# One Strassen level in the up projection, and the down projection as a stage of its own

## The chip, the cores and the metric

The kernel runs on one core of a Trainium2 chip (trn2). The time is that of the device for one launch, in microseconds (us), median of three runs. The engines are TensorE (PE; PEld are its weight loads), VectorE (DVE), ScalarE (ACT), GpSimd (POOL) and SyncE (SP), whose queue issues nearly all transfers. PE, DVE, ACT and POOL each work through a list in a fixed order; an instruction whose inputs aren't ready holds up all that stands behind it on its engine.

## The reference

One layer of a model over 1024 prompt tokens and a block of 32 sample tokens, in float32:

```python
h = _rms_norm(x, g_pre_mix)
z = h @ w_in                        # 1024 x 7424: q, k, v, HGRN2's inputs, two gates
ya = _sink_attention(...)           # windows of chunks, 16 heads
yb = _rms_norm(_hgrn2(...)) * silu(ob)
mix = sigmoid(ga) * (ya @ w_br_a) + sigmoid(gb) * (yb @ w_br_b)
x = x + _rms_norm(mix @ w_out, g_post_mix)
hf = _rms_norm(x, g_pre_ffn)
a, u = split(hf @ w_up, 2)          # 1024 x 5632
ac = b_conv + sum(ap[:, j:j + t] * w_conv[j] for j in range(3))   # ap: a behind two earlier tokens
ffn = (gelu(ac) * u) @ w_down       # 2816 x 1024
x = x + _rms_norm(ffn, g_post_ffn)
x = x + (pe @ w_ple) * sigmoid(x @ w_ple_gate)
```

The outputs are x, the last keys and values, the HGRN2 state and the last two rows of ap, for prompt and sample.

## The kernel before, in words

Activations lie by column: 128 features on the partitions, tokens along the columns. There are 1058 columns (1024 prompt, two of padding, 32 sample) in three groups of 384, 384 and 290. To keep float32's precision every factor is split into two float32r parts that add up to it, and each product of a 128x128 weight block with a group's row block is three matmuls: high x high (L189), high x low (L190), low x high (L191), in `product`. Weights go by `plan`, a list in the order of their use. `load_raw` brings a 512 KB tile into one of two raw buffers ("wr"); `load_next` makes the high part by an ACT cast (L170) and the low part by a DVE subtraction (L173).

The stages, with PE's times: attention with the gates (to about 390 us); branch B, HGRN2 (to 912); the products with w_br_a and w_br_b and the output projection (to 1208); the first up products beside the end of x1 (to 1261); ten rounds of up products of two ff tiles and down products of the two before (to about 1950); the last down products beside the per-layer product, and the gate (to the end).

Behind the output projection `z_out` copies each block and adds its squares up; `norm_sums` sums them over partitions on PE (L983), makes 1/sqrt by a chain of small DVE steps (`rsqrt`), and `norm_rows` spreads the result along the columns on PE (L291) and copies it (ACT, L293). `x1_part` then makes x1 row block by row block: two DVE operations (L1041, L1042), the split into parts (L215 on ACT, L216 on DVE), a store and a square. In the up stage `a_out` and `u_out` multiply a block by the norm, `ff_tail` does the three conv taps, gelu, the product with u and the split. `down` adds each pair of ff tiles to an accumulator in SBUF (L1157, DVE).

What sets the order: the program is written engine by engine in Python, and a scheduler orders each engine's list from it; no hand-written table. Buffers limit how far one engine can be ahead of another: six banks of PSUM for products ("mm"), two for transposes and norms ("tr").

## Time and profile before

| What | Value |
| --- | --- |
| median of three runs | 2111.21 us (2109.34 to 2114.71) |
| profiled execution, span | 2111.8 us |
| PE busy | 2086.4 us, 99% |
| DVE busy | 1249.1 us, 59% |
| ACT busy | 799.7 us, 38% |
| POOL busy | 35.7 us, 2% |
| moved by DMA | 160.22 MB, 76 GB/s |

The busy time of an engine is the time in which one of its instructions ran. Matmuls overlap, so a busy PE is read from the distance between starts. A group's row gives line, engine, operation, output and inputs, shape and count, then the busy time and the mean duration of one in ns, then the engine's idle time ahead of them and what ended it. The chain is followed back from the last instruction, at each step to what released it.

### The profile page before, as it was taken

Reading aid. Unit: us, or ns where it says so; the run is one execution under the profiler, and the core shown is the slowest. Engines: PE = TensorE matmul, PEld = TensorE weight load, DVE = VectorE, ACT = ScalarE, POOL = GpSimd, SP = SyncE. Lnnn points to the kernel's source line nnn. Section 1 sums busy time; section 2 is a strip of 40 time slices with the busy share of each in tenths; the row PEclk is TensorE's granted clock in tenths of the full one; section 3 lists DMA queues with packets and bytes.
Section 4 is the critical chain, followed back from the end, with each engine's and each line's share of the span. In section 5 each row is a group of like instructions: output and inputs, shape, how many; then the busy total and the mean of one; then the engine's idle time right before and its main releaser. Section 6 shows DMA issues by size and latency. Waiting matters only on the chain.

```text
span 2111.8 us, 34285 instructions
## 1 busy us (share of the span) xinstructions
PE 2086.4 (99%) x13292; PEld 2059.8 (98%) x13292; DVE 1249.1 (59%) x3204; ACT 799.7 (38%) x1845; POOL 35.7 (2%) x164
## 2 busy tenths in 40 slices
PE   7999999999999999999999999999999999999999
PEld 6999999999999999999999999999999999999998
DVE  6776778356666655652451684555555565556872
ACT  6555556344444444450122454321222122222532
POOL 1000000000000000000000000000000000000000
PEclk9999999999999999999999999999999999999999
DMA  7312212211111111285451221111111112111331
GB/s 223 101 63 71 81 59 71 68 41 45 55 45 48 45 53 53 77 260 165 143 189 59 83 81 40 51 50 41 41 55 46 41 41 61 41 41 53 94 109 53
DMA packets 203601, 160.22 MB, mean 76 GB/s; under 512 B 8798, under 2 KB 194417, under 8 KB 203438
## 3 DMA queue, kind: packets, MB, share of 16 engines
q1 hardware_dynamic: 203086, 157.88, 24.3%
q8 instruction: 105, 1.72, 0.3%
q14 instruction: 58, 0.48, 0.1%
q0 software_dynamic: 352, 0.15, 0.0%
HBM read 121.48 MB, written 36.51 MB: 75 GB/s over the span
## 4 chain that ended last, share of the span: by engine, by line
PE 92%; DVE 5%; DMA 2%; ACT 1%; issue 1%; SPq 0%; ACTq 0%; DVEq 0%
PE mm L189 27%; PE mm L191 27%; PE mm L190 27%; PE tr L448 1%; PE s L814 1%; PE s L421 1%; PE o L470 1%; PE o L471 1%; DVE cb L729 1%; PE s L422 1%; PE o L849 1%; PE s L806 1%; PE o L851 1%; PE tr L508 0%; DVE wl L173 0%
## 5 line engine op out<-in xcount | busy, mean ns | idle before, releaser
L189 PE MATMUL mm<-Ra,wh 128*128 128x384 f32 (+1 forms) x1632 | 531.9, 327 | 4.1 <-ACT gt L282 3.6
L191 PE MATMUL mm<-Ra,wl 128*128 128x384 f32 (+1 forms) x1632 | 529.8, 325 | 0.0
L190 PE MATMUL mm<-Rb,wh 128*128 128x384 f32 (+1 forms) x1632 | 529.4, 325 | 0.0
L189 PE MATMUL mm<-La,wh 128*128 128x384 f32 (+1 forms) x1560 | 523.5, 336 | 0.0
L191 PE MATMUL mm<-La,wl 128*128 128x384 f32 (+1 forms) x1560 | 504.4, 323 | 0.0
L190 PE MATMUL mm<-Lb,wh 128*128 128x384 f32 (+1 forms) x1560 | 503.5, 323 | 0.0
L189 PEld LDWEIGHTS mm<-Ra,wh 128*128 128x128 f32 x1632 | 307.4, 189 | 5.1 <-ACT gt L282 3.8
L190 PEld LDWEIGHTS mm<-Rb,wh 128*128 128x128 f32 x1632 | 308.1, 189 | 0.0
L191 PEld LDWEIGHTS mm<-Ra,wl 128*128 128x128 f32 x1632 | 307.3, 188 | 0.1
L189 PEld LDWEIGHTS mm<-La,wh 128*128 128x128 f32 x1560 | 294.1, 189 | 2.3 <-issue 1.6
L190 PEld LDWEIGHTS mm<-Lb,wh 128*128 128x128 f32 x1560 | 294.5, 189 | 0.2
L191 PEld LDWEIGHTS mm<-La,wl 128*128 128x128 f32 x1560 | 293.8, 188 | 0.0
L170 ACT CAST wh<-wr 128x1024 fp32r<-128x1024 f32 x137 | 143.7, 1050 | 376.9 <-PE mm L190 366.8
L173 DVE TENSOR_TENSOR wl<-wr,wh 128x1024 fp32r<-128x1024 f32 x158 | 193.1, 1223 | 100.1 <-ACT wh L170 95.8
L189 PE MATMUL mm<-act,wh 128*128 128x384 f32 (+1 forms) x528 | 171.1, 324 | 0.0
L190 PE MATMUL mm<-act,wh 128*128 128x384 f32 (+1 forms) x528 | 170.8, 324 | 0.0
L191 PE MATMUL mm<-act,wl 128*128 128x384 f32 (+1 forms) x528 | 170.7, 323 | 0.0
L1157 DVE TENSOR_TENSOR La<-La,mm 128x384 f32<-128x384 f32 (+1 forms) x240 | 122.3, 519 | 71.4 <-PE mm L191 70.5
L432 ACT ACTIVATE sc<-sc,st 128x257 f32<-128x257 f32 (+1 forms) x144 | 69.5, 484 | 92.7 <-DVE st L427 87.7
L190 PEld LDWEIGHTS mm<-act,wh 128*128 128x128 f32 x528 | 99.6, 189 | 0.0
L189 PEld LDWEIGHTS mm<-act,wh 128*128 128x128 f32 x528 | 99.4, 188 | 0.0
L191 PEld LDWEIGHTS mm<-act,wl 128*128 128x128 f32 x528 | 99.4, 188 | 0.0
(292 smaller groups left out, 2536.8 us busy)
## 6 DMA issues: line engine op xcount, KB each, us to landing
wr<-in_w_in_dram SPq DMA_DIRECT2D x58, 512.0 KB, 3.8
wr<-in_w_up_dram SPq DMA_DIRECT2D x44, 512.0 KB, 3.8
wr<-in_w_down_dram SPq DMA_DIRECT2D x22, 512.0 KB, 3.5
ya_d<-ya SPq DMA_DIRECT2D x8, 529.0 KB
x<-in_x_prompt_dram SPq DMA_DIRECT2D x8, 512.0 KB, 5.8
wr<-in_w_br_a_dram SPq DMA_DIRECT2D x8, 512.0 KB
wr<-in_w_br_b_dram SPq DMA_DIRECT2D x8, 512.0 KB, 3.8
wr<-in_w_out_dram SPq DMA_DIRECT2D x8, 512.0 KB, 5.7
```

What stands on the lines that cost most here:

```text
L170: S.copy(hi[:], raw[:])
L173: V.tensor_tensor(lo[:], raw[:], hi[:].bitcast(F32), op=ALU.subtract)
L189: E.matmul(ps, wh, a, start=first and n == 0, stop=False)
L190: E.matmul(ps, wh, b, start=False, stop=False)
L191: E.matmul(ps, wl, a, start=False, stop=last and n == len(ks) - 1)
L421: E.matmul(o, q[:, c:c + P], K1[kv][:, k0:k0 + nk], start=True, stop=False)
L422: E.matmul(o, q[:, c:c + P], K2[kv][:, k0:k0 + nk], start=False, stop=True)
L432: S.activation(sc[:m_, h, b0:e_ + 1], sc[:m_, h, b0:e_ + 1], AF.Exp, bias=st[:m_, 0, h:h + 1], scale=-1.0, accum_out=st[:m_, 1, h:h + 1])
L448: E.transpose(t[:kn, a * 256 + h * m_:a * 256 + (h + 1) * m_], sc[:m_, h, kc:kc + kn], ident[:m_, :m_])
L470: E.matmul(oc, lhs, ph[:kn, a, :2 * m_], start=a == 0, stop=False)
L471: E.matmul(oc, lhs, pl[:kn, a, :2 * m_], start=False, stop=a == len(tl) - 1)
L1157: V.tensor_tensor(dst, dst, b[:, :n], op=ALU.add)
```

## The change

- The tokens lose the two columns of padding: 1056, groups of 384, 384 and 288 up to branch B, then four groups of 264 columns (G4) for the branch products, the output and the per-layer product, and three of 352 (M3) for down and gate.
- The up projection of one ff tile of a and one of u is taken as a 2 x 2 matrix of blocks (a and u, by the halves of the 1024 features) times a 2 x 2 matrix (the halves of the features, by halves of 528 tokens), with seven products of sums of blocks. `build_ops` makes the seven operands of each half of the tokens as whole instructions of four row blocks (1056 columns); `unit_parts` makes the sums of the weights on GpSimd (four additions of 512) and their parts on ACT and DVE. A unit is 7 products x 2 x 4 row blocks x 3 = 168 matmuls of 264 columns, gathered in three accumulators X, Y, Z in PSUM; `after` takes them out.
- x1 is made four row blocks at once, and its squares are added on GpSimd (`x1_squares`). The per-layer product moves from the last down products to the place between output and up stage, and its result goes to DRAM through two buffers (tag "sq").
- The conv and gelu run on all columns at once; the result goes to DRAM (act_d). The down projection runs after all 22 units, for three groups in turn, and adds over all ff tiles in PSUM; its weights are loaded anew for each group, in 96 tiles of six or four row blocks, and `load_chunk` brings act back and splits it. The additions of L1157 are gone.

```diff
-T = 1058
-GR = ((0, 384), (384, 384), (768, 290))
+T = 1056
+GR = ((0, 384), (384, 384), (768, 288))
+H = 264
+G4 = tuple((H * g, H) for g in range(4))
+M3 = 352
...
-    def up_w(ch):
-        return [rows_cols(w_up, 0, h + f * P, P, KT) for f in (2 * ch, 2 * ch + 1) for h in (0, DFF)]
-    def down_w(ch):
-        return [rows_cols(w_down, ch * 256, c * 512, 512, 2) for c in range(2)]
-    for ch in range(NCH):
-        plan += up_w(ch)
-        if ch:
-            plan += down_w(ch - 1)
-    plan += down_w(NCH - 1)
     plan += [rows_cols(w_ple, 0, c * 512, 512, 2) for c in range(2)]
+    n_mix = len(plan)
+    KB = ((0, 6), (6, 6), (12, 6), (18, 4))
+    for _ in range(3):
+        for q in range(2):
+            plan += [rows_cols(w_down, k * P, (4 * q + c) * P, P, n) for k, n in KB for c in range(4)]
...
-    def x1_part(count=0, upto=-1):
...
+    def x1_part(g):
+        rb = oz.tile([P, H], F32, tag="rb", name=nm("rb"), bufs=2)
+        norm_rows(rss[g], T88, rb[:])
+        for i in range(2):
+            zz = z[g][:, 4 * i:4 * i + 4, :].bitcast(F32)
+            x = x1q[g][i]
+            V.tensor_tensor(zz, zz, rb[:].unsqueeze(1).to_broadcast([P, 4, H]), op=ALU.mult)
+            V.tensor_tensor(x[:], x[:], zz, op=ALU.add)
+            dma(x1_d[:, 4 * i:4 * i + 4, H * g:H * g + H], x[:])
+            for k in range(4):
+                S.mul(z[g][:, 4 * i + k, :].bitcast(F32), x[:, k, :], g_ffn[:, 4 * i + k:4 * i + k + 1])
+        x1_squares(g)
+    def x1_squares(g):
+        sq1 = fo.tile([P, H], F32, tag=f"sqz{g}", name=nm("sq1"))
+        for i in range(2):
+            for k in range(4):
+                if i == 0 and k == 0:
+                    S.activation(sq1[:], x1q[g][0][:, 0, :], AF.Square)
+                    continue
+                sq = oz.tile([P, H], F32, tag="sq", name=nm("sq"), bufs=2)
+                S.activation(sq[:], x1q[g][i][:, k, :], AF.Square)
+                G.tensor_tensor(sq1[:], sq1[:], sq[:], op=ALU.add)
+        sqz[g] = sq1
+    def build_ops(p):
+        def at(j):
+            s = where[p][j]
+            ops[p][j] = page(lq if s[0] == "l" else rp, s[1], [P, 2, 4, H], "op")
+            return ops[p][j]
+        q0, q1 = z[2 * p], z[2 * p + 1]
+        b11, b21 = q0[:, 0:4, :].bitcast(F32), q0[:, 4:8, :].bitcast(F32)
+        b12, b22 = q1[:, 0:4, :].bitcast(F32), q1[:, 4:8, :].bitcast(F32)
+        def part(j, src):
+            t = at(j)
+            S.copy(t[:, 0], src)
+            V.tensor_tensor(t[:, 1], src, t[:, 0].bitcast(F32), op=ALU.subtract)
+        part(0, b11)
+        V.tensor_tensor(b11, b11, b12, op=ALU.subtract)
+        V.tensor_tensor(b12, b12, b22, op=ALU.subtract)
+        part(6, b22)
+        V.tensor_tensor(b22, b22, b11, op=ALU.add)
+        part(1, b22)
+        part(2, b21)
+        V.tensor_tensor(b21, b21, b22, op=ALU.subtract)
+        part(3, b12)
+        part(4, b11)
+        part(5, b21)
+    def ple_product(g):
+        if not ple_w:
+            ple_w.extend((next_w(1), next_w(0)))
+        xs = pT.pop(g)
+        for c in range(8):
+            b = block(ple_w[c // 4], slice((c % 4) * P, (c % 4 + 1) * P),
+                      [xs[:, 0, k, :] for k in range(2)], [xs[:, 1, k, :] for k in range(2)],
+                      ((0, 0), (1, 1)), H)
+            t = oz.tile([P, H], F32, tag="sq", name=nm("pl"), bufs=2)
+            S.copy(t[:], b[:, :H])
+            dma(ple_d[:, c, H * g:H * g + H], t[:])
...
+        ws = [next_w(x) for x in range(4)]
+        for g in range(4):
+            for n, w in enumerate(ws):
+                z_out(4 * q + n, g, block(w, ALL, Ra[g], Rb[g], KS, H))
+                if q and g and n == 0:
+                    x1_sums(g - 1)
+                if q and g and n == 2:
+                    x1_part(g - 1)
+                if q and g == 3 and n == 1:
+                    build_ops(0)
...
+    def unit_parts(u):
+        f1, f2 = raw_w.pop(u)
+        sa = wp.tile([P, 2, 4, P], F32, tag="wb", name=nm("sa"), bufs=8)
+        sb = wp.tile([P, 2, 4, P], F32, tag="wb", name=nm("sb"), bufs=8)
+        a11, a12, a21, a22 = f1[:, 0:4, :], f1[:, 4:8, :], f2[:, 0:4, :], f2[:, 4:8, :]
+        s1, s2, s3, s4 = sa[:, 0], sa[:, 1], sb[:, 0], sb[:, 1]
+        def parts(src):
+            t = wp.tile([P, 2, 4, P], F32R, tag="wb", name=nm("wt"), bufs=8)
+            S.copy(t[:, 0], src)
+            V.tensor_tensor(t[:, 1], src, t[:, 0].bitcast(F32), op=ALU.subtract)
+            ready_w.append(t)
+        parts(a11)
+        yield
+        G.tensor_tensor(s1, a21, a22, op=ALU.add)
+        G.tensor_tensor(s2, a11, s1, op=ALU.add)
+        parts(s2)
+        yield
+        parts(a12)
+        yield
+        G.tensor_tensor(s3, a11, a21, op=ALU.add)
+        parts(s3)
+        yield
+        parts(s1)
+        yield
+        parts(a22)
+        yield
+        G.tensor_tensor(s4, a12, s2, op=ALU.add)
+        parts(s4)
...
+    prepare(1)
+    p_cols(0)
+    for g in range(4):
+        if g < 3:
+            p_cols(g + 1)
+        ple_product(g)
+        if g == 0:
+            x1_sums(3)
+            x1_part(3)
+        if g == 1:
+            build_ops(1)
+    octx.close()
...
-    def up(ch):
...
-    def down(ch, act, sums=None):
...
+        V.tensor_tensor(u, u, rbT[:], op=ALU.mult)
+        V.tensor_tensor(u[:, 0:1024], a[:, 0:1024], u[:, 0:1024], op=ALU.mult)
+        V.tensor_tensor(u[:, 1024:T], a[:, 1026:1058], u[:, 1024:T], op=ALU.mult)
+        dma(act_d[f][:], u)
...
+        def mults(i, t, first, ps):
+            n = 7 * u + i
+            if i not in w:
+                w[i] = ready_w[n]
+            for p in ps:
+                for k in range(4):
+                    wh, wl = w[i][:, 0, k, :], w[i][:, 1, k, :]
+                    xh, xl = ops[p][i][:, 0, k, :], ops[p][i][:, 1, k, :]
+                    o = t[:, p, 0:H]
+                    E.matmul(o, wh, xh, start=first and k == 0, stop=False, skip_group_check=True)
+                    E.matmul(o, wh, xl, start=False, stop=False, skip_group_check=True)
+                    E.matmul(o, wl, xh, start=False, stop=k == 3, skip_group_check=True)
+        def v(t, ps):
+            return t[:, ps[0]:ps[-1] + 1, 0:H]
+        def after(i, ps):
+            x, y, zz = v(X, ps), v(Y, ps), v(Z, ps)
+            sl = slice(ps[0], ps[-1] + 1)
+            if i == 0:
+                S.copy(s1c[:, sl], x)
+            elif i == 1:
+                V.tensor_tensor(U2[:, sl], s1c[:, sl], y, op=ALU.subtract)
+            elif i == 2:
+                V.tensor_tensor(ab[:, 2:2 + T].rearrange("p (a h c) -> p a h c", a=2, h=2)[:, sl, 0, :],
+                                x, rb4[:, sl, 0, :], op=ALU.mult)
+            elif i == 3:
+                V.tensor_tensor(nU3[:, sl], y, s1c[:, sl], op=ALU.subtract)
+            elif i == 4:
+                V.tensor_tensor(us4[:, sl, 1, :], nU3[:, sl], zz, op=ALU.subtract)
+            elif i == 5:
+                V.tensor_tensor(us4[:, sl, 0, :], y, s1c[:, sl], op=ALU.subtract)
+            else:
+                V.tensor_tensor(t12[:, sl], U2[:, sl], zz, op=ALU.add)
...
+        order = ((0, X), (1, Y), (2, X), (3, Y), (4, Z), (5, Y), (6, Z))
+        first = (0, 1, 4)
+        for ps in (((0,), (1,)) if u == 0 else ((0, 1),)):
+            for i, t in order:
+                prepare(7 * u + i + AHEAD)
+                mults(i, t, i in first, ps)
+                after(i, ps)
...
+    def load_chunk(g, i):
+        k0, n = KB[i]
+        hi, lo = (page_at(s, [P, 6, M3], "ac") for s in chunk_at[i])
+        for k in range(n):
+            dma(lo[:, k, :].bitcast(F32), act_d[k0 + k][:, M3 * g:M3 * g + M3])
+        for k in range(0, n, 2):
+            src = lo[:, k:k + 2, :].bitcast(F32)
+            S.copy(hi[:, k:k + 2, :], src)
+            V.tensor_tensor(lo[:, k:k + 2, :], src, hi[:, k:k + 2, :].bitcast(F32), op=ALU.subtract)
+        chunk[i] = (hi, lo)
...
+    for g in range(3):
+        for q in range(2):
+            bs = [mm_bank() for _ in range(4)]
+            for i, (k0, n) in enumerate(KB):
+                hi, lo = chunk[i]
+                for c in range(4):
+                    product(bs[c][:, :M3], next_w(), ALL, [hi[:, k, :] for k in range(n)],
+                            [lo[:, k, :] for k in range(n)], tuple((k, k) for k in range(n)),
+                            i == 0, i == 3)
+                    if i == 3:
+                        d_out(g, 4 * q + c, bs[c])
+                if q == 1 and g < 2:
+                    load_chunk(g + 1, i)
```

The first place is PE's list around the norm of the last but one group behind the output projection. Before (L983 are the sums, L291 the rows, `nr` is 1/rms; about 50 products of the first up blocks stand between the two):

```order
L191 MATMUL mm_13520<-Ra_13179,wl_12941 128x384
L983 MATMUL tr_13482<-ones,sqz_12541 128x1 x2
L983 MATMUL tr_13482<-ones,sqz_12541 34x1
L189 MATMUL mm_13520<-Ra_13179,wh_12940 128x384
...
L190 MATMUL mm_13631<-Rb_13180,wh_13353 128x384
L291 MATMUL tr_13607<-ident,nr_13484 128x128 x2
L291 MATMUL tr_13607<-ident,nr_13484 128x34
L191 MATMUL mm_13631<-Ra_13179,wl_13354 128x384
```

And after, on the same engine (L982 the sums, L293 the rows of group 2; mm_14279 is the last output block, `pr` the per-layer input, `pc` its parts by column):

```order
L194 MATMUL mm_14279<-Ra_11980,wl_13601 128x264
L982 MATMUL tr_14131<-ones,sqz_13102 88x1 x3
L293 MATMUL tr_14237<-ident,nr_14133 128x88 x3
L1097 MATMUL tr_14327<-ident,pr_14322 128x88 x3
L1097 MATMUL tr_14333<-ident,pr_14322 128x88 x3
L192 MATMUL mm_14356<-pc_14326,wh_13606 128x264
L192 MATMUL mm_14366<-pc_14326,wh_13606 128x264
```

The rows of the norm no longer have products between them and the sums.

The second place is DVE's list in the same stretch. Before (`rst` and `nr` are the steps of the norm, the others x1's row blocks):

```order
L1041 SCALAR_TENSOR_TENSOR La_12534<-La_12534,gph,rb_13421 128x384
L204 SCALAR_TENSOR_TENSOR rst_13492<-rsb_13491 128x3
L985 TENSOR_SCALAR nv_13546<-tr_13545 128x3
L205 TENSOR_TENSOR rst_13492<-rst_13492,nv_13483 128x3
L216 SCALAR_TENSOR_TENSOR Rb_13428<-La_12534,gvec,Ra_13427 128x384
L206 SCALAR_TENSOR_TENSOR nr_13484<-rst_13492,rsb_13491 128x3
L997 TENSOR_TENSOR sq_2236_13429<-sq_2236_13429,sq_13509 128x384
```

And after (L1076 and L1067 are the sums and the low parts of the up operands `op`, made from z):

```order
L985 TENSOR_SCALAR nv_14132<-tr_14131 88x1
L1076 TENSOR_TENSOR z_13090<-z_13090,z_13091 128x1056
L203 TENSOR_SCALAR rsb_14140<-nv_14132 128x3
L1012 TENSOR_TENSOR sqz_13103<-sqz_13103,sq_14179 128x264
L204 TENSOR_SCALAR rsb_14140<-rsb_14140 128x3
L1067 TENSOR_TENSOR op_14191<-z_13091,op_14191 128x1056
L207 SCALAR_TENSOR_TENSOR rst_14141<-rsb_14140 128x3
L1067 TENSOR_TENSOR op_14198<-z_13091,op_14198 128x1056
L208 TENSOR_TENSOR rst_14141<-rst_14141,nv_14132 128x3
L1067 TENSOR_TENSOR op_14201<-z_13090,op_14201 128x1056
L209 SCALAR_TENSOR_TENSOR nr_14133<-rst_14141,rsb_14140 128x3
```

The steps of the norm now alternate with instructions of 1056 columns instead of 384.

The third place is ACT's list at the per-layer product's copies. Before, beside the last down products (L1231 the copies, kept in SBUF; y is the gate):

```order
L1231 COPY ple_20762<-mm_20813 128x290
L212 CAST Ra_20475<-La_14048 128x384
L1231 COPY ple_20762<-mm_20827 128x290
L996 ACTIVATE sq_20720<-La_14050 128x290
L996 ACTIVATE sq_20745<-La_14050 128x290
L293 COPY rb_20698<-tr_20699 128x384
```

And after, between the last copy of group 0 and the first copies of group 1 (L1112 the copies, L1035 the scalings of x1 of group 3, L1043 and L1046 the squares, L1066 the casts of operands):

```order
L1112 COPY pl_14433<-mm_14426 128x264
L1035 ACTIVATE z_13093<-x_2276_13917,gvec 128x264 x3
L1035 ACTIVATE z_13093<-x_2277_13919,gvec 128x264 x4
L1043 ACTIVATE sq_2368_14478<-x_2276_13917 128x264
...
L1066 CAST op_14617<-z_13092 128x1056
L1046 ACTIVATE sq_14498<-x_2277_13919 128x264
L1112 COPY pl_14525<-mm_14518 128x264
L1066 CAST op_14607<-z_13093 128x1056
L1112 COPY pl_14535<-mm_14528 128x264
```

The copies that free PE's banks stand behind x1's scalings and the operands' casts.

More of the change, by code (lines that the diff above doesn't have):

```diff
@@ L1003, in layer_kernel @@
[L1003 to L1014 removed]
+    z = [page(lq, g, [P, 8, H], "z") for g in range(4)]
@@ L1120, in up @@
[L1120 to L1131 removed]
+        n = T + 2
+        a = fp.tile([P, T + 2], F32, tag="a", name=nm("a"), bufs=2)
@@ new lines, in layer_kernel, with page_at @@
+    for u in range(NF):
+        up_unit(u)
+    chunk_at = (("l4", "r3"), ("l6", "r5"), ("l7", "r6"), ("r0", "r7"))
+    def page_at(s, shape, name):
+        return page(lq if s[0] == "l" else rp, s[1:], shape, name)
+    chunk = {}
+    def load_chunk(g, i):
[8 more added lines that the diff above has]
+        chunk[i] = (hi, lo)
@@ L1315 @@
+            x2_part(0, g)
+            for c in range(4):
+                if q == 0 and g == 0 and c == 0:
+                    x2_start(2)
+                if q == 0 and g == 0 and c == 2:
+                    x2_rows(2)
+                b = block(ws[c], ALL, xh[g], xl[g], KS, M3)
+                x2_part()
+                late.append((g, 4 * q + c, y_out(g, 4 * q + c, b)))
+                if len(late) > 1:
+                    y_done(*late.pop(0))
+    for l in late:
+        y_done(*l)
 _INS = ['x_prompt', 'x_sample', 'cache_win_k', 'cache_win_v', 'state_hgrn', 'cache_ffn_conv',
```

617 lines of the change are left out of this document (275 added, 342 removed).

## The prediction

> **What bounds the kernel now.** I read the page's engine line first, then the span in slices, then the chain that ended last.
>
> ```profile
> span 2111.8 us, 34285 instructions
> PE 2086.4 (99%) x13292; PEld 2059.8 (98%) x13292; DVE 1249.1 (59%) x3204; ACT 799.7 (38%) x1845; POOL 35.7 (2%) x164
> ...
> PE   7999999999999999999999999999999999999999
> ...
> DVE  6776778356666655652451684555555565556872
> ACT  6555556344444444450122454321222122222532
> ...
> PEclk9999999999999999999999999999999999999999
> ...
> PE 92%; DVE 5%; DMA 2%; ACT 1%; issue 1%; SPq 0%; ACTq 0%; DVEq 0%
> ```
>
> TensorE is busy in every slice but the first, at full clock, and 92% of the chain is PE. Work taken from PE is time taken from the span, as long as nothing else makes PE wait. The table by stage shows where a helper could become that:
>
> ```profile
> 912.00:1208.00 296.00, 292.42 (x1804) 291.87 (x1802) 126.42 (x238) 82.06 (x154) 0.20 (x2) 0.99 0.48 145
> 1208.00:1261.00 53.00, 53.00 (x337) 52.35 (x337) 47.85 (x142) 27.43 (x52) 0.00 (x0) 1.00 0.28 92
> 1261.00:1950.00 689.00, 689.00 (x4265) 689.00 (x4264) 379.24 (x709) 173.07 (x269) 2.01 (x20) 1.00 0.15 46
> ```
>
> (Start and end, length, then busy time of PE, PEld, DVE, ACT, POOL, then clock, DMA share, GB/s.) Between 1208 and 1261 us, where the output projection hands over to the first up products, DVE is busy 47.85 of 53 us and PE still does not wait. That stage is the narrow place. In the 689 us of up and down chunks, DVE is at 55%.
>
> **Prices.** Matmuls are pipelined, so the spacing of starts counts, not the recorded 0.34 us.
>
> ```profile
> 1499.83 0.34 PE L191 MATMUL mm<-Ra,wl 128*128 128x384 f32 x1
> ...
> 1503.17 0.29 PE L189 MATMUL mm<-Ra,wh 128*128 128x290 f32 x1
> ...
> 1503.98 0.30 PE L189 MATMUL mm<-Ra,wh 128*128 128x290 f32 x1
> ```
> ```profile
> 301.23 0.28 PE L470 MATMUL o<-ph,Vs 128*128 128x256 f32 x1
> 301.35 0.28 PE L471 MATMUL o<-pl,Vs 128*128 128x256 f32 x1
> 301.47 0.27 PE L470 MATMUL o<-ph,Vs 128*128 128x256 f32 x1
> ```
>
> From 1499.83 to 1503.17 there are 19 starts of 384 columns: 0.1758 us each. Then 6 of 290 columns in 0.81 us: 0.135. A product of 256 columns takes 0.12. Between these, 264 columns are worth 0.123 us and 352 columns 0.162; a triple over all tokens costs 2 x 0.1758 + 0.135 = 0.4866 us before, 4 x 0.123 = 0.492 in four groups of 264, and 3 x 0.162 = 0.486 in three of 352.
>
> ```profile
> L173 DVE TENSOR_TENSOR wl<-wr,wh 128x1024 fp32r<-128x1024 f32 x158 | 193.1, 1223 | 100.1 <-ACT wh L170 95.8
> ...
> L213 DVE TENSOR_TENSOR pl<-tr,ph 128x512 fp32r<-128x512 f32 x56 | 38.0, 688 | 2.8 <-ACT ph L212 1.9
> ...
> L1157 DVE TENSOR_TENSOR La<-La,mm 128x384 f32<-128x384 f32 x160 | 86.7, 552 | 55.6 <-PE mm L191 55.6
> ...
> L1157 DVE TENSOR_TENSOR La<-La,mm 128x290 f32<-128x290 f32 x80 | 35.6, 455 | 15.8 <-PE mm L191 14.9
> ...
> L205 DVE TENSOR_TENSOR rst<-rst,nv 128x3 f32<-128x3 f32 x27 | 4.2, 157 | 0.2
> ```
> ```profile
> 1206.59 0.56 DVE L1042 TENSOR_TENSOR La<-La,xT 128x384 f32<-128x384 f32 x1
> 1207.05 0.46 DVE L997 TENSOR_TENSOR sqz<-sqz,sq 128x290 f32<-128x290 f32 x1
> 1207.42 0.56 DVE L1042 TENSOR_TENSOR La<-La,xT 128x384 f32<-128x384 f32 x1
> ```
> ```profile
> 1207.17 0.62 ACT L215 ACTIVATE Ra<-La,gvec 128x384 fp32r<-128x384 f32 x1 [1.26 <-DVE La L1042]
> 1207.70 0.51 ACT L993 ACTIVATE sq<-La 128x384 f32<-128x384 f32 x1
> 1208.11 0.60 ACT L215 ACTIVATE Ra<-La,gvec 128x384 fp32r<-128x384 f32 x1
> ```
>
> A two-input DVE operation lasts about 0.15 us plus 1.05 ns a column (1223, 688, 455 ns), and the next independent one starts some 0.09 us before it ends (0.46 after 0.56). So DVE passes 1056 columns in 1.18 us, 1024 in 1.14, 512 in 0.60, 264 in 0.35. ACT passes 384 columns with a scale in 0.53 and without in 0.41; scaled, 264 take 0.42 and 0.32, and 1056 plain ones about 1.0. A step that depends on the one before pays all of its 0.157.
>
> **The change, part by part.**
>
> Up products. Before: 44 weight tiles x 24 x 0.4866 = 513.8 us. After: 22 units x 168 products x 0.123 = 454.6. Gain 59.2. The three projections in groups of 264: 24 tiles x 24 x (0.492 - 0.4866) = +3.1; the per-layer product +0.3; 58 input tiles without two columns about -1.2; down and gate at 0.486 instead of 0.4866: nothing. PE in all: **-57**, with +1 for a fourth group's norm and more small transposes.
>
> The 240 additions of L1157 (86.7 + 35.6 = 122.3 us of DVE) leave. DVE was covered there, so that is worth nothing by itself; it makes room for the new evacuations.
>
> Up units in steady state. Each takes PE 168 x 0.123 = 20.7 us. DVE does, in that time, 7 weight remainders of 512 (4.2), 6 evacuations of 528 (3.7), the last pieces L1277 and L1280 (0.8), three copies (0.3), two taps of 1058 (2.5), two products with the norm and u (2.4): 13.9 us, 67%. The kernel before shows PE without a wait at 55%. What is new is GpSimd with four additions of 512 a unit. No row has a two-input GpSimd operation; the nearest are these:
>
> ```profile
> 9.93 0.31 POOL L570 TENSOR_SCALAR_AFFINE_SELECT cm<-cm 128x128 f32<-128x128 f32 x1
> 10.17 0.19 POOL L377 MEMSET qa<- 128x96 f32 x1
> ```
>
> 0.24 us from start to start for 128 columns with one input, so 512 need 0.7 (as on DVE) to 1.9 us (twice 0.96), or 3 to 8 us a unit: GpSimd itself keeps up. If DVE stood still meanwhile it would need 17 to 22 of 20.7 us, so a unit loses 0 to 0.7 us. I take 0.3 in most units, near the lower end because 13.9 leaves room: **+8** with the first unit's half products, bounds 0 and +15.
>
> Hand-over from the output projection to the up stage. Here whole four-block instructions of 1056 columns and the seven operands of each half (11 instructions of 1.18 for each half) come onto DVE, and PE's order shows nothing to do beside them. I follow PE.
>
> (a) Behind the last output block stand L982 and L293 of group 2 with no product between. L982 waits for the last square of group 2. From the norm rows of group 1 (L293, with 3.1 blocks or 9.2 us of PE still to come) DVE has eight instructions of 1056, two of 1024 and one of 264 to pass, with 0.46 for the copy of the rows: 9.4 + 2.3 + 0.35 + 0.46 = 12.5. PE waits 3.5 at least, 9 if DVE also waits for ACT's 18 scalings, squares and casts. Between L982 and L293 DVE has five more of 1056 (5.9), two of 264 (0.7), three of 512 (1.8) and the 12 small steps, of which the last stand alone (1.5): 9.9, up to 12. I take 6.5 + 11 = **17.5**, bounds 13.5 and 21.
>
> (b) The first per-layer product waits for its lower parts, which are put behind four x1 instructions: 0.46 + 4 x 1.18 + 0.7 = 5.9, less 1.3 of transposes and five first products: **+4.6**, bounds 3 and 7.
>
> (c) Per-layer products have six banks; their copies stand in ACT's order behind the x1 scalings, squares and casts. Group 0: 8 x 0.42 + 9 x 0.32 + 2 x 1.0 + 0.6 = 8.9 and DVE's 2.4 ahead of them, against PE's lead of 1.3 + 6 x 0.74 = 5.7: about 5. Group 1: from L293 of group 3, 0.46, four x1 instructions 4.7, the last scalings 1.7, six of the second half's operands 7.1, a cast and a copy 2, in all 16, against PE's 4: 12. Together **+17**, bounds 8 and 22.
>
> (d) The copies go out to DRAM through two buffers:
>
> ```profile
> ta_d<-gt SPq DMA_DIRECT2D x16, 192.0 KB, 2.1
> ```
>
> With 0.4 for the copy and a little under 2.1 for 132 KB a buffer turns in about 2.4 us, a block in 1.2, where PE needs 0.74: for groups 2 and 3, 16 x 0.46 = 7.4, and a backlog of about five blocks that the first up product waits for, since it takes the same banks: **+13**, bounds 5 and 18. Smaller waits (sums of groups 0 and 3): **+3**, 0 to 6.
>
> The hand-over: 55, bounds 30 and 74.
>
> Down stage. The weights come three times, through two raw buffers. The gate stage before shows such a ring's turn:
>
> ```profile
> 1999.96 1.14 DVE wl L173
> ...
> 2001.13 4.37 DMA wr<-in_w_ple_gate_dram
> ...
> 2005.52 1.06 ACT wh L170
> ...
> 2006.62 0.44 PE mm L189
> ```
>
> 1.14 + 4.37 + 1.06 and the gaps make 6.6 us for a buffer, 3.3 for a tile of 512 KB. The new tiles have 384 KB (72 of them) and 256 KB (24). If the load shrinks nearly with its size (3.6 and 2.9), a tile comes every 2.7 and 2.0 us, and PE needs 18 x 0.162 = 2.92 and 1.94: covered but for a little. If loads stay at 4.37, since act chunks travel beside them, it is 3.0 and 2.8: 72 x 0.1 + 24 x 0.9 = 29 us. I take **+6**, bounds 0 and 29, near the lower end because a load with less to move has no row that makes it as slow as a full one. The cover is the ring itself; were it gone, each late tile would stop PE at once, since four banks wait for it. Stores of act, loads of chunks and x1 go on SP's queue; their issues stand between weight loads, and that is in the same bounds. Moving the per-layer product ahead leaves the end of the kernel shorter of work, not longer, and I cost it at nothing.
>
> Sum: -57 + 1 + 8 + 55 + 6 = +13 us. The span is 2111.8 us, and the median of the three runs 2111.21, so one execution stands for them. **2124 us.**
>
> A rule that could change this: the Trainium skill, page "SBUF — State Buffer", section "SBUF: two separate sides", says that GpSimd and a DVE instruction with two inputs in SBUF exclude each other for a whole instruction. By its page "GPSIMD Engine Reference", section 3.1, an addition of 2048 columns takes GpSimd 4497 ns, so 264 would be an estimated 0.6 us. No row of this trace shows two-input work on GpSimd beside DVE. By the two together the 28 additions of squares in the hand-over would be taken out of DVE's time there, some 17 us, and the sum would be +30 instead of +13.
>
> **The rivals.**
>
> 1. Faster. The waits of the hand-over hide each other: PE, stopped in (a), lets DVE and ACT run ahead, and then (c) and (d) find their banks empty. For it: in the same place before, 47.85 of 53 us of DVE were hidden, and the chains in (c) start from work that (a) has already delayed. Against it: the order puts (b) and (c) behind x1 work that cannot start before L293. Left would be the serial minimum of (a), 13.5, and 8 for the rest: -57 + 1 + 21.5 + 0 + 0 = -34.5, **2077 us**. It decides once the hand-over costs less than 42 us.
>
> 2. GpSimd holds DVE up, in the hand-over and in the units. In the hand-over 28 additions of 264 at 0.24 / 128 x 264 = 0.5 to twice that: 14 to 28 us, of which DVE has nearly no slack to absorb any. In the units up to +15 instead of +8. About +13 + 20 + 7 = +40, **2151 us**. For it: the hand-over's squares are waited for by ACT in order. Against: POOL's rows before are too short to show anything.
>
> 3. The down stage is bound by its ring: +29 instead of +6, **2147 us**. For it: the gate stage before waits on the same ring (the DMA of 4.37 above was in the chain); against: smaller tiles.
>
> 4. No change: the hand-over at 45 and the rest near its lower ends, **2111 us**.
>
> That the change does not do what it says is no rival: the order has 168 products of 264 columns for each unit.
>
> **How the numbers follow.** My case 0.38; rival 1: 0.25; rival 2: 0.15; rival 3: 0.10; rival 4: 0.12. Runs before differ by 5.4 us, so about 0.3% (6.3 us) is what can be told from no change. Slower: 0.38 + 0.15 + 0.10 = 0.63; same 0.12; faster 0.25. The predicted time is that of my case, whose own range is 2112 to 2138. The range for all cases reaches from 2074, a little below rival 1's time, to 2160, a little above rival 2's; that leaves out some 0.1 at each end.
>
> **What the profile after would show.** PE in the up stage: starts of 264 columns 0.123 us apart and a unit every 21 us; if 0.135 or more, the gain is 10% of 455 us smaller. Idle time of PE just before L982 and L293 of group 2 (17 us), released by DVE; before the per-layer products, released by ACT; before the first up product. In the units DVE near 67% busy and PE's wait under 0.7 us. In the down stage, waits of PE on casts of weights below 10 us in all. I am wrong if the hand-over has under 42 us of PE's idle time, or if GpSimd's additions take over 2 us each.

## The result

The changed kernel takes 2135.24 us (median of four runs, 2134.1 to 2138.28), the kernel before 2111.1: 1.011 times as long, 95% interval 1.009 to 1.0129. The profiled execution spans 2133.8 us.

The page of the changed kernel:

```profile
span 2133.8 us, 37571 instructions
...
PE 2042.0 (96%) x14474; PEld 2007.0 (94%) x14474; DVE 1318.4 (62%) x3131; ACT 902.3 (42%) x2029; POOL 195.3 (9%) x264
...
PE   7999999999999999999999567999999999999998
...
PEclk9999999999999999999999778999999999999999
...
PE 78%; DVE 8%; DMA 6%; issue 3%; ACT 3%; POOL 1%; SPq 0%; ACTq 0%; DVEq 0%; POOLq 0%
```

PE is busy for 44 us less than before, and the span is 22 us longer. Slices 23 to 25, from about 1174 to 1334 us, are where it went: PE is half busy, and its granted clock falls with it. That is the hand-over from the output projection to the up stage. Who ends PE's waits there (engine and line that waits, who ended it, us in total, times, longest):

```profile
PE mm L192 <- ACT pl L1112: 18.6, 4, 12.0
PE tr L293 <- DVE nv L980: 11.7, 2, 10.7
PE tr L982 <- DVE sqz L1012: 11.6, 3, 8.7
PE st L1249 <- ACT pl L1112: 7.4, 1, 7.4
PE tr L1097 <- DVE pc L216: 3.2, 1, 3.2
```

Between two up products in the steady state (first and tenth of a row of starts):

```profile
1499.83 0.29 PE L1249 MATMUL st<-op,wt 128*128 128x264 f32 x1
...
1500.92 0.28 PE L1249 MATMUL st<-op,wt 128*128 128x264 f32 x1
```

Nine starts in 1.09 us: 0.121 us for 264 columns. In parts of the hand-over the same size starts only every 0.22 us, called half pace here:

```profile
1238.40 0.42 PE L192 MATMUL mm<-pc,wh 128*128 128x264 f32 x1
1238.62 0.42 PE L193 MATMUL mm<-pc,wh 128*128 128x264 f32 x1
```

It is the clock: the profile grants 0.50 from 1185.0 to 1188.3 us and from 1262.0 to 1266.8, and 1.00 from 1188.5 to 1199. Half pace follows waits. PE was idle for 2.2 us up to 1183.55 us, ran 1.4 us at full pace and then 3.3 us at half pace; after the wait that ended at 1261.78 half pace lasted 5.1 us. Summed over all starts from 1175 us to the end of the first unit (the first pair of ff tiles in the up stage), products took 14.1 us more than at 0.121, and the waits were 58.9 us. Such sums of waits are taken here from one start of PE to the next, less one product; the idle time that the profile gives, as in the list above, is 56.5 us in the same stretch.

The account of the 24 us, from the first product of the branch stage to the end (1195.5 us before, 1219.5 after): a unit of the up stage has a pitch of 20.35 us. Before, a triple over all tokens took 0.485 us on the mean from 1261 to 1950 us (the prediction's row gave 0.4866), so that a unit's worth took 44 x 24 x 0.485 / 22 = 23.28: -64. Products of 352 columns start 0.160 us apart, a triple 0.480, which gives some -4 in down and gate. The waits of the hand-over and the half pace: +73. One wait in the second unit: +1. The down stage: 12 us of waits, and some 4 for half pace behind them: +16. The columns of padding give -1 and more, and the kernel before lost 2 us to half pace and short waits in these stages itself. That makes about +19; the last 5 are not assigned. The account adds up PE's time. It doesn't show that each term, taken away alone, would shorten the kernel by its size; that is what the experiments are for.

### The profile page after: what moved, and what is told of

It is laid out like the page before. It is cut to its first block, busy times and chain, and to the rows that moved or that the text cites. A ratio compares the mean times of both kernels' runs of the same rounds, so it can differ in the third digit from the quotient of the medians.

```text
span 2133.8 us, 37571 instructions
## 1 busy us (share of the span) xinstructions
PE 2042.0 (96%) x14474; PEld 2007.0 (94%) x14474; DVE 1318.4 (62%) x3131; ACT 902.3 (42%) x2029; POOL 195.3 (9%) x264
## 4 chain that ended last, share of the span: by engine, by line
PE 78%; DVE 8%; DMA 6%; issue 3%; ACT 3%; POOL 1%; SPq 0%; ACTq 0%; DVEq 0%; POOLq 0%
PE mm L192 16%; PE mm L193 16%; PE mm L194 16%; PE st L1251 6%; PE st L1249 6%; PE st L1250 6%; DMA wr<-in_w_down_dram 3%; DVE wl L176 1%; PE tr L449 1%; POOL sq L1047 1%; PE s L815 1%; ACT wh L173 1%; PE s L422 1%; PE o L471 1%; DVE cb L730 1%
## 5 line engine op out<-in xcount | busy, mean ns | idle before, releaser
L192 PE MATMUL mm<-La,wh 128*128 128x384 f32 (+1 forms) x1368 | 458.8, 336 | 0.0
L1249 PE MATMUL st<-op,wt 128*128 128x264 f32 x1232 | 349.8, 284 | 8.6 <-ACT pl L1112 7.4
L1251 PE MATMUL st<-op,wt 128*128 128x264 f32 x1232 | 351.0, 285 | 0.0
L1250 PE MATMUL st<-op,wt 128*128 128x264 f32 x1232 | 349.0, 283 | 0.0
L176 DVE TENSOR_TENSOR wl<-wr,wh 128x1024 fp32r<-128x1024 f32 (+2 forms) x188 | 198.0, 1053 | 175.6 <-ACT wh L173 171.0
L173 ACT CAST wh<-wr 128x1024 fp32r<-128x1024 f32 (+2 forms) x167 | 149.4, 895 | 283.4 <-DMA wr<-in_w_down_dram 119.5
L1249 PEld LDWEIGHTS st<-op,wt 128*128 128x128 f32 x1232 | 232.7, 189 | 9.1 <-ACT pl L1112 7.7
L1250 PEld LDWEIGHTS st<-op,wt 128*128 128x128 f32 x1232 | 232.7, 189 | 0.0
L1251 PEld LDWEIGHTS st<-op,wt 128*128 128x128 f32 x1232 | 232.1, 188 | 0.0
L192 PE MATMUL mm<-ac,wh 128*128 128x352 f32 x528 | 172.0, 326 | 3.2 <-ACT wh L173 3.2
L194 PE MATMUL mm<-ac,wl 128*128 128x352 f32 x528 | 171.4, 325 | 2.9 <-DVE wl L176 2.6
L193 PE MATMUL mm<-ac,wh 128*128 128x352 f32 x528 | 170.1, 322 | 0.0
L192 PE MATMUL mm<-Ra,wh 128*128 128x264 f32 x512 | 146.4, 286 | 1.1 <-ACT gt L284 1.1
L193 PE MATMUL mm<-Rb,wh 128*128 128x264 f32 x512 | 145.8, 285 | 0.0
L194 PE MATMUL mm<-Ra,wl 128*128 128x264 f32 x512 | 145.7, 285 | 0.0
```

Source lines behind the costliest of these rows:

```text
L173: S.copy(hi[:], raw[:])
L176: V.tensor_tensor(lo[:], raw[:], hi[:].bitcast(F32), op=ALU.subtract)
L192: E.matmul(ps, wh, a, start=first and n == 0, stop=False)
L193: E.matmul(ps, wh, b, start=False, stop=False)
L194: E.matmul(ps, wl, a, start=False, stop=last and n == len(ks) - 1)
L1249: E.matmul(o, wh, xh, start=first and k == 0, stop=False, skip_group_check=True)
```

## The experiments

The profiles are compared by three stretches: from the first branch product to the first up product, to the last up product, to the end. The first varies less than the whole, since the runs start that stage 909 to 920 us into the span.

| Kernel | to first up product | up stage | to the end | time, us |
| --- | --- | --- | --- | --- |
| changed | 381.5 | 456.4 | 381.6 | 2135.24 |
| squares on DVE | 376.0 | 456.8 | 389.1 | 2137.49 |
| places for per-layer products | 359.8 | 460.0 | 384.7 | 2120.67 |
| added products | 382.1 | 456.8 | 386.1 | 2139.02 |
| third raw buffer | 382.0 | 456.4 | 366.0 | 2118.44 |
| third buffer, squares on DVE | 377.8 | 454.9 | 366.6 | 2112.61 |
| third buffer, up sums on DVE | 380.9 | 456.0 | 367.4 | 2114.16 |
| third buffer, no squares | 355.3 | 456.3 | 366.2 | 2092.01 |
| third buffer, places | 359.3 | 458.8 | 366.2 | 2097.91 |
| third buffer, added products | 383.9 | 454.8 | 366.5 | 2121.39 |
| all repairs | 354.1 | 458.2 | 366.6 | 2091.91 |
| all repairs, added products | 354.8 | 459.8 | 364.5 | 2092.04 |

**Squares on DVE.**

```diff
-                G.tensor_tensor(sq1[:], sq1[:], sq[:], op=ALU.add)
+                V.tensor_tensor(sq1[:], sq1[:], sq[:], op=ALU.add)
```

> The changed kernel with the squares of x1 (line 1047, 28 additions of 264 columns) added on DVE instead of GpSimd. Theory GpSimd-chain: in the hand-over these additions took 0.76 us alone and up to 1.65 us beside two-input DVE work, ACT's squares wait for them and the operands' casts and the copies of the per-layer product stand behind those; without them PE's idle time between 1181 and 1301 us falls from 59 us to about 52, and with some of the lost clock back the time falls by 6 to 10 us, to 2125 to 2129. Rival DVE-bound: DVE is the limit of the hand-over, and 28 x 0.35 = 10 us more on it lengthen it: 2140 to 2146.

Measured: 2137.49 us, ratio to before 1.012 (1.0095 to 1.0145). The first up product came 5.5 us sooner, but the stretch behind the last up product was 7.5 us longer: PE's waits in the down stage were 20.1 us here and 11.6 in the profile of the changed kernel. The time lies between the two forecasts and decides neither theory; the down stage had to be quieted first.

**A third raw buffer for the down weights.**

```diff
-        raws.append(wp.tile([P, kt, n], F32, tag="wr", name=nm("wr"), bufs=2))
+        third_ring = len(raws) >= n_mix + 16 and (len(raws) - n_mix) % 3 == 2
+        pool, tag, bufs = (ring3[0], "wr3", 1) if third_ring else (wp, "wr", 2)
+        raws.append(pool.tile([P, kt, n], F32, tag=tag, name=nm("wr"), bufs=bufs))
...
-            yrs[g] = ep.tile([P, 3, 256], F32, tag="yr", name=nm("yr"), bufs=4)
+            yrs[g] = ep.tile([P, 3, 256], F32, tag="yr", name=nm("yr"), bufs=3)
```

> The changed kernel with a third raw buffer for the down weights (from the 17th tile on; one buffer less for rows of the output, in the gate stage). Theory ring: PE's 12 us of waits in the down stage come from the turn of two raw buffers (load, cast, subtraction); with three they fall below 3 us, and the time by 8 to 10 us, to 2125 to 2128. Rival transfers: the loads are slow because act chunks, x1 and weights share the DMA engines (0.6 busy there); then a third buffer changes under 3 us.

Measured: 2118.44 us, 1.0026 times before (1.0011 to 1.0041), 17 us faster than the changed kernel: more than either theory said. PE's waits in the down stage before the edit (`wh` and `wl` are the parts of the down weights, `sqd` the squares for the norm behind it), and after it:

```profile
PE mm L192 <- ACT wh L173: 3.2, 6, 1.1
PE tr L982 <- DVE sqd L1344: 2.7, 1, 2.7
PE mm L194 <- DVE wl L176: 2.6, 6, 0.5
```

```profile
PE tr L985 <- DVE sqd L1348: 0.8, 1, 0.8
PE tr L296 <- DVE nr L212: 0.4, 1, 0.4
```

So the ring of two buffers was the limit, not the transfers alone. The waits on weights lay between 1821 and 1846 us and between 1929 and 1936, where `load_chunk` brings act for the next group: there the casts and the subtractions came late. With the third buffer the stretch to the end is 364.5 to 367.4 us in all kernels, 15.6 shorter here than in the changed kernel. About 10 of it are waits; the half pace behind them (3.7 us from 1935.72 and 5.4 from 2026.20 in the changed kernel) is likely a part of the rest.

**The squares again, with the third buffer.**

> Squares of x1 on DVE instead of GpSimd again, this time with the third raw buffer, so that the down stage's waits (11.6 to 20.1 us in the profiles so far) do not cover the result. Theory GpSimd-chain: 2118.4 - 6.6 = about 2112 us. Rival: the earlier start of the up stage was a matter of the one profile, 2116 to 2121.

Measured: 2112.61 us, ratio to before 0.9997 (0.9985 to 1.0009). That is what the GpSimd theory gave: 5.8 us less than with the third buffer alone. DVE got 28 more additions and the hand-over was shorter, so it is not DVE's load that sets it. The rows show how it goes. GpSimd in the changed kernel:

```profile
L1159 POOL TENSOR_TENSOR sa<-wu,sa 128x512 f32<-128x512 f32 x22 | 46.0, 2089 | 1.7
L1047 POOL TENSOR_TENSOR sq<-sq,sq 128x264 f32<-128x264 f32 x28 | 31.7, 1133 | 842.2 <-ACT sq L1046 840.6
L1158 POOL TENSOR_TENSOR sa<-wu 128x512 f32<-128x512 f32 x22 | 29.9, 1359 | 210.8 <-PE st L1251 196.4 <-ACT wt L1153 9.1 <-DVE wt L1154 5.2
```

ACT, behind such an addition each time (in brackets its idle time and what ended it):

```profile
1257.91 0.42 ACT L1046 ACTIVATE sq<-x 128x264 f32<-128x264 f32 x1 [1.29 <-POOL sq L1047]
1258.24 1.05 ACT L1066 CAST op<-z 128x1056 fp32r<-128x1056 f32 x1
1259.63 0.42 ACT L1046 ACTIVATE sq<-x 128x264 f32<-128x264 f32 x1 [0.34 <-POOL sq L1047]
1261.35 0.38 ACT L1112 COPY pl<-mm 128x264 f32<-128x264 f32 x1 [1.29 <-POOL sq L1047]
```

With two places for the squares, ACT makes one square for each addition, and the copy that frees PE's bank stands at the end of that row. In all, ACT stood idle for 11.5 us behind GpSimd's additions between 1181 and 1301 us. DVE's instructions beside GpSimd's also took longer there, an estimated 5 us together (nine additions of 264 columns 0.67 us on the mean instead of 0.43, four sums of 1056 columns 1.7 to 2.0 instead of 1.25). The edit takes away most of both, so how much of the 5.8 us either one holds isn't shown.

**Places for the per-layer products.**

```diff
-    ple_w = []
+    ple_w, pages = [], []
...
-            t = oz.tile([P, H], F32, tag="sq", name=nm("pl"), bufs=2)
-            S.copy(t[:], b[:, :H])
-            dma(ple_d[:, c, H * g:H * g + H], t[:])
+            if c == 0:
+                pages.append(page(*((rp, 5), (rp, 7), (lq, 2), (lq, 3))[g], [P, 8, H], "pl"))
+            t = pages[-1][:, c, :].bitcast(F32)
+            S.copy(t, b[:, :H])
+            dma(ple_d[:, c, H * g:H * g + H], t)
```

> The changed kernel with eight places for each group's per-layer products (in pages of SBUF that are free there) instead of two buffers shared with the squares. Theory buffers: the copies wait for the stores of the two buffers, which costs PE part of the wait in group 1, the waits in groups 2 and 3 and the 7.4 us before the first up product: 17 us of idle time less, and some clock back, 2110 to 2118. Rival order: the copies come late because they stand behind x1's scalings and the operands' casts in ACT's order; the buffers then change less than 4 us, 2131 to 2139.

Measured: 2120.67 us (ratio to before 1.0035, 1.0021 to 1.0049), 14.6 less than the changed kernel, a smaller gain than the theory of the buffers forecast (2110 to 2118 us) and a far larger one than its rival's. The first up product came 21.7 us sooner. In the hand-over of the changed kernel ACT had waited most of all for the stores out of the two buffers:

```profile
ACT pl L1112 <- DMA ple_d<-pl: 19.7, 14, 4.7
```

With the places that wait is gone. PE's longest waits then:

```profile
PE tr L293 <- DVE nv L980: 11.1, 3, 10.7
PE mm L192 <- ACT pl L1114: 11.0, 2, 10.5
PE tr L982 <- DVE sqz L1012: 10.0, 2, 7.8
PE tr L1097 <- DVE pc L216: 5.8, 2, 3.2
PE st L1251 <- ACT Sp L1262: 3.1, 1, 3.1
```

The wait in front of the first up product (7.4) and those of the small copies are gone; one of 10.5 on a copy is left, that of group 1. So more than half of the 26 us that PE waited for copies was the two buffers, and the order on ACT is the likely rest. Part of the gain came back: the last line is a new wait in the first unit, where ACT's copy (L1262) waits 3.9 us for a store of these places, and the stretch of the up stage grew from 456.4 to 460.0 us. With the third raw buffer as well:

> Places for the per-layer products and the third raw buffer, squares still on GpSimd. If the 22.9 us that the places brought forward stand by themselves: 2118.4 - 22.9 = 2095.5 us, within 4; then the squares on DVE add only 4 us in the kernel with all repairs (2091.9), not 6.6. Rival: part of them came back as waits of the down stage in that profile, 2099 to 2106.

Measured: 2097.91 us, 0.9934 (0.992 to 0.9948), 20.5 less than with the third buffer alone, as the first theory said.

**Squares left out.** Of the eight squares of x1 in each group seven are left out here, with their additions; the norm ahead of the up projection is that of one row block.

```diff
                 if i == 0 and k == 0:
                     S.activation(sq1[:], x1q[g][0][:, 0, :], AF.Square)
-                    continue
+                continue
```

> With the third raw buffer, and seven of the eight squares of x1 of each group (ACT) with their additions (GpSimd) left out, so that the norm ahead of the up projection is that of one row block. Theory: the squares stand in ACT's order ahead of the operands' casts and of the per-layer copies, so the first up product comes 20 to 28 us sooner, 2090 to 2098 us. Rival, DVE-bound: the hand-over is set by DVE's 1056-column instructions, which are all still there; under 8 us sooner.

Measured: 2092.01 us, 26 less than with the third buffer alone. DVE's 1056-column instructions were all there, so they alone don't set the hand-over. PE's waits in front of the norm's sums and rows fell to 8.1 us, from 25.5 in the changed kernel. The squares also share the two buffers of the per-layer copies, so this run doesn't tell ACT's order from the use of the buffers.

**Up sums on DVE.** The four sums of each unit's weights (s1 to s4) are made by V instead of G.

> With the third raw buffer, the four sums of up weights of each unit on DVE instead of GpSimd. If GpSimd's additions (1.3 to 2.1 us each) hold DVE up in the units, DVE without them would be no busier and the units no longer; if DVE has room for 4 x 0.6 us more, the pitch of a unit stays at 20.35 us either way, and the time is 2115 to 2120. Rival: DVE is at its limit with 90% of a unit, and the pitch rises to 20.6 or more, 2124 or later.

Measured: 2114.16 us, 1.0002 times before (0.999 to 1.0014), some 4 us less than with the third buffer alone. The edit isn't shown to have brought these 4 us: the three stretches of the two profiles sum up to the same 1204 us, and 2.3 us of the difference lie ahead of the branch stage. The pitch of a unit stayed at 20.35 us. From 1400 to 1700 us (busy time of PE, PEld, DVE, ACT, POOL), first this kernel, then the changed one:

```profile
1400.00:1700.00 300.00, 300.00 (x2479) 300.00 (x2478) 246.47 (x417) 106.36 (x148) 1.49 (x15) 1.00 0.25 79
```

```profile
1400.00:1700.00 300.00, 300.00 (x2479) 300.00 (x2478) 232.93 (x354) 106.40 (x149) 90.24 (x74) 1.00 0.25 79
```

DVE took the sums at 82% with PE never waiting. Its busy time rose by only 13.5 us, though 60 additions of 0.69 us, 41 us of work, came onto it. The reason is in its longest instructions, the two conv taps of a unit, with the sums on GpSimd (L1224 and L1225) and on DVE (L1227 and L1228):

```profile
L1225 DVE SCALAR_TENSOR_TENSOR a<-ab,cvec,a 128x1058 f32<-128x1058 f32 x22 | 47.5, 2160 | 0.7
L1224 DVE SCALAR_TENSOR_TENSOR a<-ab,cvec,a 128x1058 f32<-128x1058 f32 x22 | 39.0, 1773 | 12.4 <-ACT a L1223 12.4
```

```profile
L1227 DVE SCALAR_TENSOR_TENSOR a<-ab,cvec,a 128x1058 f32<-128x1058 f32 x22 | 29.1, 1321 | 1.3 <-ACT a L1226 1.2
L1228 DVE SCALAR_TENSOR_TENSOR a<-ab,cvec,a 128x1058 f32<-128x1058 f32 x22 | 29.0, 1316 | 0.0
```

The taps run beside GpSimd's additions and take 1.3 us more in each unit. So GpSimd does hold DVE up in the units, but DVE has room for it: PE waited once, 1.2 us in the second unit, and not at all with the sums on DVE.

**Added products.** 220 products (138 in the last of the three kernels) whose results are thrown away stand in PE's waits.

```diff
+    def idle_work(n, d=None):
+        d = d or tr_bank()
+        for _ in range(n):
+            E.matmul(d[:, :H], ws[3][0][:, 0, :], Ra[3][0], start=True, stop=True)
```

> The changed kernel with 220 more products of 264 columns whose results are thrown away (about 27 us at full clock), put into PE's waits of the hand-over: 60 before the last output block, 80 behind the sums of group 2, 80 before the seventh per-layer block of group 1. Theory clock: PE's granted clock falls after its idle stretches (0.22 us from start to start of a product of 264 columns instead of 0.121), which costs 14 us; with PE kept busy the clock stays up, and the time falls by 6 to 12 us, to 2123 to 2129, though PE has more to do. Rival: the clock falls for another reason, or idle time is all that counts; then the time stays, or rises by what the added products delay, 2134 to 2150.

> The 220 thrown-away products in the waits again, now with the third raw buffer. In the first such run the first up product came 2.3 us sooner than without them, though PE had 26.6 us more to do, and products at half pace took 14.3 us of real work instead of 27.3; the time was covered by the down stage's waits. Theory clock: 2 to 7 us below the kernel with the third buffer alone (2118.4), 2111 to 2116 us. Rival: the added products delay as much as the clock gives, 2117 to 2121.

> The kernel with all repairs (2091.9 us), with 138 thrown-away products of 264 columns in the two waits that are left around the sums of group 2 (13 and 5 us): 100 ahead of the sums, 38 behind them. Theory clock: behind these waits about 7 us of products ran at half pace, so 3 us come back, 2087 to 2090. Rival: no gain, or a loss where the products do not end before the norm is ready, 2091 to 2098.

Measured: 2139.02 us; with the third buffer 2121.39 (without them 2118.44); with all repairs 2092.04 (without them 2091.91). The stretch to the first up product was 382.1, 383.9 and 354.8 us, against 381.5, 382.0 and 354.1 without them. So the added products gained nothing, though PE's waits there fell from 58.9 to 38.2 us in the first and from 37.5 to 21.0 in the last. The clock did rise in the first: from 1181 to 1320 us the granted clock was 0.88 instead of 0.74, and the time did not fall, since PE had 26.6 us more to do. In the last, products lost 11.3 us to half pace instead of 8.4: the waits that were left, some 2 to 4 us each, were again followed by half pace. The theory that the lost clock can be bought back with thrown-away products so falls. That half pace follows waits stays as an observation; how much shorter the hand-over would be at full clock, nothing here shows, since a slower PE ahead of a wait may only shorten that wait.

**All repairs.** Squares on DVE, places, third raw buffer, and the squares of the last group behind the per-layer products.

> All repairs together: squares of x1 added on DVE, eight places for each group's per-layer products, a third raw buffer for the down weights from the 17th tile on, and the squares of the last group of x1 put behind the per-layer products. Separately these brought the first up product forward by 6.6 us (squares on DVE) and 22.9 us (places), and shortened the part behind the last up product from 381.6 to 366.0 us (third buffer). Theory that they are separate waits: 2118.4 - 22.9 - 6.6 = 2089 us, within 5, which is 1% faster than the kernel before. Rival that the first two remove the same wait: 2095 to 2100.

Measured: 2091.91 us, 0.99 times before (0.9883 to 0.9916): 1% less than the kernel before, and 2% less than the changed one. PE's longest waits in its hand-over:

```profile
PE tr L985 <- DVE sqz L1015: 13.5, 2, 13.2
PE tr L1101 <- DVE pc L219: 6.2, 2, 3.2
PE tr L296 <- DVE nv L983: 5.8, 3, 5.3
```

The hand-over still holds 37.5 us of waits. The effects add up nearly: 2118.44 - 20.5 - 5.8 = 2092. The fourth edit, the moved squares of the last group, has no run of its own; this sum leaves nothing for it.

## Why the prediction was right, and where its terms were off

The direction and the cause were right: the up stage gained more than 2% of the span, and the hand-over took it back. Forecast 2124, measured 2135; it lay in the range, and near the upper end of my case's own (2112 to 2138). That the sum came so close is in part luck, as its terms show:

- *Up products, -59.* Too small: a product of 264 columns takes 0.121 us, not 0.123, and the gain was 64. The price was read off a line between single rows of 256 and 290 columns, and the product lies below that line.
- *(a), 17.5.* The waits in front of L982 and L293 of group 2 were 8.7 and 10.7 us by the profile. The order was read rightly: the steps of the norm stand between instructions of 1056. These rows are DVE's in that stretch:

```profile
1209.59 2.18 DVE L1076 TENSOR_TENSOR z<-z,z 128x1056 f32<-128x1056 f32 x1
...
1215.90 1.25 DVE L1067 TENSOR_TENSOR op<-z,op 128x1056 fp32r<-128x1056 f32 x1
...
1219.70 0.16 DVE L209 SCALAR_TENSOR_TENSOR nr<-rst,nr 128x3 f32<-128x3 f32 x1
```

- *(b), 4.6.* 3.2 us by the profile.
- *(c) and (d), 17 and 13.* PE waited 18.6 and 7.4 us for copies, 26 where 30 was forecast. The division was wrong: (c) put its part down to ACT's order alone, while the two buffers held more than half of all: with places for the products 11.0 was left.
- *The hand-over's 55.* Its waits were 58.9 us. What was left out is half pace, 14.1 us more of PE's time. The trace before showed it once, behind the 3.6 us wait at the start of the branch stage:

```profile
917.67 0.52 PE L190 MATMUL mm<-Rb,wh 128*128 128x384 f32 x1
917.99 0.52 PE L191 MATMUL mm<-Ra,wl 128*128 128x384 f32 x1
```

  Products of 384 columns start 0.32 us apart here, not 0.176, from 917.67 to 920.87 us. The prediction read the clock by slices of 53 us, in which this can't be seen, and said that the clock was full. In PE's account this is the term that was missing; no run shows that the time would fall by as much without it. The Trainium skill, page "TensorE: Matmul & The Clock Gate", section "HAM oscillation — how this bites in real kernels", has the rule for it: idle gaps over some 3.4 us bring PE back to half its clock. The runs agree in kind, but here an idle time of 2.2 us was followed by half pace too, in some kernels and not in others.
- *Up units, +8.* PE waited 1.2 us in all units behind the first, near the lower bound that the price of GpSimd left open. DVE was busy for 78% of a unit, not for the 67% of the prediction; two thirds of the difference are the conv taps beside GpSimd (1.3 of 20.35 us).
- *Down stage, +6.* It was 16, between the bounds 0 and 29. The loads landed in 3.4 and 2.7 us, nearly as priced; the waits came where act chunks travelled beside them, and half pace behind them was left out again. The waits on casts and subtractions of weights stayed below 10 us, as forecast (3.2 and 2.6 us).
- *Rival 2, GpSimd.* In the hand-over it held, but small: 6 us, not 20. The rule of the Trainium skill on the shared port (page "SBUF — State Buffer", section "SBUF: two separate sides"), weighed in the prediction, agrees with the rows: an addition of 264 columns took 0.76 us alone (where 0.6 was estimated) and 1.65 beside DVE's two-input work, and the DVE row of 2.18 us above ran beside GpSimd's L1159, where its like takes 1.25. The chain through ACT was a part of the price that the prediction named only in passing. In the units the taps were held up and PE was not, but for 1.2 us.
- *The sign for GpSimd.* The prediction called itself wrong if GpSimd's additions took over 2 us each. One kind did (L1159, 2.09 us on the mean), and it cost next to nothing: with the sums on DVE the pitch stayed the same. The sign was badly chosen, since the duration of an instruction says little where its engine and its neighbour have room.
- *Rival 3, the ring.* Partly true as well: 16 to 17 us of the 29. *Rival 1* (waits that hide each other) did not come.

Together: -12 for the shorter products (in projections, down and gate too), -7 for the units, +4 for the waits of the hand-over, +14 for half pace, +10 for the down stage. That is 9 of the 11 us between 2124 and 2135: the sum came close because terms of both signs were off.

## What to carry to other kernels

When a stage's products are made cheaper by sums of operands, the sums have to be made somewhere: count them at the border to the stage before, where they meet the norm, and not only in the steady state. Two buffers between a copy and a store, shared with a second use, cost 15 to 20 us here, and a ring of two for the weights 17: together more than the whole net loss of 24. Places that lie free for a few microseconds are worth looking for. And a wait of PE was often followed by some microseconds at half pace; look for it between single starts, not in slices of 50 us.

## What the runs showed of the hardware

- Behind many of PE's waits, products started 0.22 us apart instead of 0.121 (264 columns), for 3.3 us and 5.1 in the two cases above, at a granted clock of 0.50. The length of one wait doesn't decide it. The idle time of 2.2 us in front of the norm's sums (L982) at the beginning of the hand-over was followed by half pace in the changed kernel (1183.55 us), and not in the one with places (1183.7) nor with the first added products (1181.3). Idle times of 2.7, 2.9 and 3.0 us at 916.8, 915.8 and 1243.9 us (added products with the third buffer, places with the third buffer, all repairs) were followed by a granted clock of 1.00. All longer ones behind the HGRN2 stage had half clock beside them or within 2 us. Filling part of such waits with thrown-away products saved no time in three pairs of kernels.
- Two-input additions on GpSimd took 0.76 us for 264 columns and 1.3 for 512, 1.8 to 1.9 times DVE's 0.43 and 0.69. The second of two dependent sums took 2.09 on the mean, beside DVE's conv taps, which took 1.77 and 2.16 us there and 1.32 without GpSimd beside them.
- PE's waits in the down stage, the same code in the kernels without the third buffer, were 11.6 us in one profile and 20.1 in another; with the third buffer they nearly vanished. Why they differ so stays open.
